# Output projections of two attentions split by heads, with sums, casts and subtractions put in another order

## The chip, the core and the metric

The kernel runs on one core of one Trainium2 chip. The metric is the time of one execution on the device in microseconds (us). Matmuls run on TensorE (PE in the profile), elementwise work on VectorE (DVE) and ScalarE (ACT); transfers from memory are started by SyncE (SP). Each engine takes its own instructions in a fixed order and waits, at the head of that order, for what an instruction needs.

## What is computed

Two transformer layers on 512 tokens of width 1024 in float32. Layer 0 has differential attention with 8 heads (the kernel calls two heads a pair), layer 1 sliding-window attention with 16 heads over 4 key/value heads and a learned sink. Each attention is followed by an output projection that is added to the stream x, then a normalization and a gated feed-forward block. Cut to what the change touches:

```python
a = p[:, :, 0] - lam * p[:, :, 1]                      # layer 0, per head
o = rms_norm(einsum('bhqk,bkhe->bqhe', a, v), subln) * (1.0 - lambda_init)
x = x + o.reshape(B, S, DA_V) @ w_o                    # "first end" below
h = rms_norm(x, ffn_norm[0]); x = x + swiglu(h, w_gate_up[0], w_down[0])
...
o = einsum('bnhgqk,bnkhd->bnqhgd', p, vw)              # layer 1, per unit
x = x + o.reshape(B, S, SW_HEADS * HEAD_DIM) @ sw_w_o  # "second end" below
h = rms_norm(x, ffn_norm[1]); x = x + swiglu(h, w_gate_up[1], w_down[1])
```

## The kernel before, in words

**Precision.** A float32 operand is kept as two tiles, a high part `hi` (a cast on ACT) and the rest `lo` (a subtraction on DVE, `src - hi`). `mm3` (L295 to L298) multiplies with three matmuls into one bank: hi by hi, hi by lo, lo by hi. So nearly every operand costs a cast on ACT and a subtraction on DVE before PE may use it. For activations that come out of a bank, `split_evac` (L300 to L303) does both; for weights, `load_w` (L280 on) does: one transfer (L287) into a tile `raw`, then a cast (L269) and a subtraction (L270) for each half. There are two `raw` buffers, so the transfer of a third piece starts when both subtractions of the first are done.

**Output projection.** `o_units` (L453) loads the four pieces of half of an output matrix, in the order (0,0), (0,1), (2,0), (2,1): the first number says which two of the half's four row blocks, the second which 512 columns. `o_block` (L457) makes one block of 128 tokens: for each half of the columns one bank, four `mm3`, and a sum on DVE that adds the bank to `xs`, the stream (L468). The first bank so needs the first and the third piece.

**Layer 0.** Four pairs of heads follow one another; `DA_STEPS3` is the table of places at which the last pair's steps (scores, weighted sum U, its weights W, norm N, and B, the spread of the inverse root `ro` over a bank by four small transposes, L1148) are put between the projection's matmuls. For pair 3 the projection of half 0 (pairs 0 and 1) fills first, then half 1 (pairs 2 and 3) for blocks 0 and 1; blocks 2 and 3 follow behind the table. The softmax of a block of tokens ends in four Exp on ACT (L1084) and two mixes on DVE (L1092); the mixed `s` is transposed (L1108) and split into `aT` (L302, L303) for the weighted sum. Then `ffn.norm(t)` (L520 on: Square on ACT, inverse root in small steps on DVE, two products `xn`, L532) and `ffn.turn(t)` (L534: two transposes of four 128x128 blocks, split into `hTh` and `hTl`) make block t ready for the feed-forward, whose `start` (L594 on) first multiplies blocks 0 and 1 (256 columns).

**Layer 1.** 16 units, each 4 heads on 128 queries, have five steps: turn the queries, scores, two transposes of the softmax (`turn_p`, L1439, split into `ph` and `pl`) and `weigh` (12 matmuls into `po`, split into `oh` and `ol`). `SW_AT` holds the five places of each unit. Units 14 and 15 end the table; the projection of token block 3 and the feed-forward of layer 1 follow.

**Order.** PE's order is that of the code. The order on ACT and DVE is made by a scheduler before the launch, from priorities (`high_priority`) and from the order in which things are written; `issue_after` forbids it to put an instruction ahead of a named one. SP starts transfers in its own order.

## Time and profile before

| | |
|---|---|
| three runs | 1122.44, 1122.76 and 1123.15 us, median 1122.76 |
| the profiled execution | 1122.68 us |
| its span (first to last instruction) | 1120.6 us |
| mean granted TensorE clock | 0.998 of full speed |
| busy share of PE, DVE, ACT, POOL | 98%, 90%, 63%, 5% |
| first end (last pair, projection) | about 225 to 270 us |
| second end (units 14 and 15, projection) | about 763 to 784 us |

The span lies 2.1 us below the time of its own execution. In a row of the timeline stand the start, the duration of one instruction (or of several alike from the first start to the last end), engine, line, operation, what it writes and reads, its shape, and in brackets how long the engine was idle before it and what released it. Durations of matmuls overlap: the distance from one start to the next is what a matmul takes on PE. The same holds on DVE and ACT for instructions that follow one another closely.

### The profile page before, as it was taken

The numbers are of one execution on the slowest core, as the hardware profiler recorded it, in microseconds if no ns is written. First come the engines' busy times: TensorE is split into PE (matmuls) and PEld (weight loads), VectorE is DVE, ScalarE is ACT, GpSimd is POOL, SyncE is SP. The second block draws the span as 40 slices with busy tenths as digits, with TensorE's granted clock in tenths as the row PEclk, the third lists the DMA queues.
The fourth block names the chain that finished last, engine by engine and source line by source line (L and its number), as shares of the span: only waits on it lengthen the run. The fifth ranks groups of instructions, "written<-read, shape, count | busy, mean of one in ns | idle before, by whom it ended". The sixth has DMA issues, their size and how long they took to land.

```text
span 1120.6 us, 20161 instructions
## 1 busy us (share of the span) xinstructions
PE 1101.9 (98%) x7206; PEld 979.5 (87%) x7206; DVE 1007.9 (90%) x2418; ACT 709.4 (63%) x1575; POOL 54.6 (5%) x76
## 2 busy tenths in 40 slices
PE   9999999999999999999999999999999999999998
PEld 7878888778989989989998778778989999998997
DVE  5979798979999999999998787988899999899997
ACT  5565756454556675675677499697555675566574
POOL 0100000000000010010003000000010000000000
PEclk9999999999999999999999999999999999999999
DMA  6312121224453444336124311120545247246213
GB/s 199 113 57 76 39 77 48 67 69 137 151 158 100 143 87 156 114 84 199 58 48 106 112 39 57 39 76 26 198 136 168 76 104 213 79 104 178 77 30 103
DMA packets 94085, 114.90 MB, mean 103 GB/s; under 512 B 5993, under 2 KB 70914, under 8 KB 93986
## 3 DMA queue, kind: packets, MB, share of 16 engines
q1 hardware_dynamic: 87216, 100.97, 28.0%
q0 software_dynamic: 6720, 12.65, 6.3%
q8 instruction: 56, 0.92, 0.3%
q14 instruction: 43, 0.35, 0.1%
q10 hardware_dynamic: 50, 0.01, 0.0%
HBM read 99.98 MB, written 2.10 MB: 91 GB/s over the span
## 4 chain that ended last, share of the span: by engine, by line
PE 81%; DVE 12%; ACT 6%; issue 1%; POOL 0%; DVEq 0%; ACTq 0%; POOLq 0%
PE acc L725 18%; PE tr L725 12%; PE tr L813 10%; PE acc L813 8%; PE acc L296 8%; PE acc L297 7%; PE acc L298 7%; PE po L725 2%; ACT s L1420 2%; PE tr L439 2%; DVE hss L389 1%; ACT s L1427 1%; DVE lo L270 1%; DVE u L405 1%; PE po L813 1%
## 5 line engine op out<-in xcount | busy, mean ns | idle before, releaser
L589 ACT CAST hi<-r 128x512 fp32r<-128x512 f32 x160 | 98.9, 620 | 78.9 <-PE acc L725 34.2
L296 PE MATMUL acc<-hi,hTh 128*128 128x512 f32 (+1 forms) x352 | 133.1, 378 | 2.2 <-DVE vl L1029 2.2
L297 PE MATMUL acc<-lo,hTh 128*128 128x512 f32 (+1 forms) x352 | 124.4, 354 | 0.4 <-DVE lo L270 0.4
L298 PE MATMUL acc<-hi,hTl 128*128 128x512 f32 (+1 forms) x352 | 124.4, 354 | 0.0
L589 ACT CAST hi<-g 128x512 fp32r<-128x512 f32 x154 | 94.9, 618 | 40.6 <-PE acc L297 19.2
L591 DVE TENSOR_TENSOR lo<-r,hi 128x512 fp32r<-128x512 f32 x160 | 104.8, 685 | 5.8 <-ACT hi L589 5.4
L589 ACT CAST hi<-raw 128x512 fp32r<-128x512 f32 x108 | 66.9, 620 | 61.5 <-PE tr L725 19.0
L796 ACT CAST ah<-lf 128x256 fp32r<-128x256 f32 x154 | 61.2, 404 | 47.2 <-PE tr L813 14.7
L725 PE MATMUL acc<-hTh,lo 128*128 128x256 f32 x288 | 81.5, 283 | 0.0
L725 PE MATMUL acc<-hTl,hi 128*128 128x256 f32 x288 | 81.5, 283 | 0.0
L725 PE MATMUL acc<-hTh,hi 128*128 128x256 f32 x288 | 81.4, 283 | 0.0
L725 PE MATMUL acc<-tl,hi 128*128 128x256 f32 x288 | 81.1, 282 | 0.0
L725 PE MATMUL acc<-th,hi 128*128 128x256 f32 x288 | 81.1, 281 | 0.0
L725 PE MATMUL acc<-th,lo 128*128 128x256 f32 x288 | 81.0, 281 | 0.0
L296 PEld LDWEIGHTS acc<-hi,hTh 128*128 128x128 f32 x352 | 66.9, 190 | 12.9 <-issue 2.6
L269 ACT CAST hi<-raw 128x512 fp32r<-128x512 f32 x96 | 57.4, 619 | 30.8 <-PE acc L298 17.6
L591 DVE TENSOR_TENSOR lo<-g,hi 128x512 fp32r<-128x512 f32 x110 | 75.2, 684 | 1.5 <-ACT hi L589 1.4
L298 PEld LDWEIGHTS acc<-hi,hTl 128*128 128x128 f32 x352 | 66.8, 190 | 9.5
L588 POOL DMA_DIRECT2D lo<-g x44 | 38.5, 975 | 715.1 <-ACT lo L587 308.4
L297 PEld LDWEIGHTS acc<-lo,hTh 128*128 128x128 f32 x352 | 67.1, 191 | 6.7 <-DVE lo L270 0.7
L591 DVE TENSOR_TENSOR lo<-raw,hi 128x512 fp32r<-128x512 f32 x108 | 72.7, 685 | 0.0
L270 DVE TENSOR_TENSOR lo<-raw,hi 128x512 fp32r<-128x512 f32 x96 | 64.4, 684 | 6.7 <-ACT hi L269 6.3
(278 smaller groups left out, 3635.0 us busy)
## 6 DMA issues: line engine op xcount, KB each, us to landing
r<-in_w_gate_up_dram SPq DMA_DIRECT2D x80, 512.0 KB, 4.9
g<-in_w_down_dram SPq DMA_DIRECT2D x88, 256.0 KB, 5.3
lo<-g POOLq DMA_DIRECT2D x44, 256.0 KB, 3.8
raw<-in_da_w_qkv_dram SPq DMA_DIRECT2D x30, 256.0 KB, 3.1
raw<-in_da_w_qkv_dram SPq DMA_DIRECT2D x8, 512.0 KB, 4.0
raw<-in_da_w_o_dram SPq DMA_DIRECT2D x8, 512.0 KB, 3.7
raw<-in_w_gate_up_dram SPq DMA_DIRECT2D x8, 512.0 KB, 3.7
raw<-in_sw_w_o_dram SPq DMA_DIRECT2D x8, 512.0 KB, 3.7
```

Of the source, the lines that this page charges most:

```text
L269: nc.scalar.copy(hi, part)
L270: nc.vector.tensor_tensor(lo, part, hi.bitcast(F32), op=ALU.subtract)
L296: nc.tensor.matmul(dst, sh, mh, start=start, stop=False)
L297: nc.tensor.matmul(dst, sh, ml, start=False, stop=False)
L298: nc.tensor.matmul(dst, sl, mh, start=False, stop=stop)
L439: nc.tensor.matmul(banks[c][:, cols], q[a][rows], k[b][rows], start=a + b == 0, stop=a == 1)
L588: nc.gpsimd.dma_start(out=lo.bitcast(F32), in_=src, accum_op=ALU.add)
L589: nc.scalar.copy(hi, src)
L591: nc.vector.tensor_tensor(lo, src, hi.bitcast(F32), op=ALU.subtract)
L725: nc.tensor.matmul(dst, l[:, k, :], r[:, k, :], start=fresh and k == 0 and i == 0, stop=k == 3 and i == 2, skip_group_check=not fresh)
L796: nc.scalar.copy(ah, src)
L813: nc.tensor.matmul(bank, l[:, tk], r, start=fresh and i == 0 and n == 0, stop=i == len(qs) - 1 and n == 2, skip_group_check=not fresh)
```

## The change

At the first end: the sums of two blocks of half 0, the casts and the subtractions of the four pieces of half 1 are held back, by `issue_after`. The sum (2, 1) waits for `rooted`, the step that makes `ro` for the first half of the tokens; the sum (3, 0) for `mixed`, the last mix of pair 3; the weights' casts for `raised`, the last Exp of pair 3, and their subtractions for `rooted`. Block 2 of half 1 is made with both banks open (`o_block2`): first the row blocks of pair 2 into both, then those of pair 3. The last B of `DA_STEPS3` goes one `mm3` later.

At the second end: `weigh` of unit 14 goes ahead of the first `turn_p` of unit 15 (two numbers of `SW_AT`: 77.7403 becomes 77.62 and 78.1612 becomes 77.64), `weigh` of unit 15 goes behind the first half of the first bank of the last projection block, which is `o_block2` too; `turn(0)` and `turn(1)` go behind one and two more `mm3` of that block's end; `norm(2)` is issued behind the last cast of unit 15, `norm(3)` as before behind the block. In PE's order it reads: `weigh` 14, `turn_p` 15 twice, half of bank 0, `weigh` 15, half of bank 1, `turn(0)`, the rest of bank 0, one `mm3` of bank 1, `turn(1)`, the last `mm3`.

```diff
--- before.py
+++ after.py
@@ -108,13 +108,13 @@
         (42.8, W, 1, 0),
         (43.3, W, 1, 1),
         (48.6, N, 1),
-        (56.9, B, 1),
+        (58.6, B, 1),
     ]
 
 
 DA_FILL3 = 0.4757
 SW_K = [11.4, 13, 18.5, 22]
...
 SW_R = [24.5925, 29, 34.7335, 50, 54, 60.3794]
 SW_F = 57.2488
 SW_BOOST = 51
@@ -247,7 +247,8 @@
             else:
                 eng.tensor_tensor(w, y, y, op=ALU.mult)
                 eng.scalar_tensor_tensor(w, w, -0.5, v, op0=ALU.mult, op1=ALU.mult)
-            eng.scalar_tensor_tensor(dst if it == 2 else y, w, 1.5, y, op0=ALU.add, op1=ALU.mult)
+            last = eng.scalar_tensor_tensor(dst if it == 2 else y, w, 1.5, y, op0=ALU.add, op1=ALU.mult)
+        return last
 
     class Split:
 
@@ -299,8 +300,9 @@
 
     def split_evac(hi, lo, src):
         with tc.high_priority(offset=pri["evac"]):
-            nc.scalar.copy(hi, src)
+            cast = nc.scalar.copy(hi, src)
             nc.vector.tensor_tensor(lo, src, hi.bitcast(F32), op=ALU.subtract)
+        return cast
 
     def new_hT():
         hh = xp.tile([P, KT, S], F32R, name=nm("hTh"), tag="hTh", bufs=1)
@@ -454,7 +456,7 @@
         return {(j, n): load_w([wv[:, k0 + j:k0 + j + 2, n * 512:(n + 1) * 512]], 2, 512)
                 for j in (0, 2) for n in range(2)}
 
-    def o_block(units, pieces, t, ready=None):
+    def o_block(units, pieces, t, ready=None, after=lambda t, n: None):
         while ready and not ready():
             yield None
         for n in range(2):
@@ -464,8 +466,24 @@
                 mm3(pt, sh, sl, *units[j - j % 2, n].row(j % 2), j == 0, j == 3)
                 yield 0.65
             xsl = xs[:, t, n * 512:(n + 1) * 512]
-            with tc.high_priority(offset=HOT):
+            with tc.high_priority(offset=HOT), ExitStack() as hold:
+                if after(t, n):
+                    hold.enter_context(tc.issue_after(after(t, n)))
                 nc.vector.tensor_tensor(xsl, xsl, pt, op=ALU.add)
+
+    def o_block2(units, pieces, t, order):
+
+        banks = {}
+        for n, half in order:
+            if n not in banks:
+                banks[n] = acc()
+            for j in (2 * half, 2 * half + 1):
+                mm3(banks[n], *pieces(j, t), *units[2 * half, n].row(j % 2), j == 0, j == 3)
+                yield n, j
+            if half:
+                xsl = xs[:, t, n * 512:(n + 1) * 512]
+                with tc.high_priority(offset=HOT):
+                    nc.vector.tensor_tensor(xsl, xsl, banks[n], op=ALU.add)
 
 
     class Flow:
@@ -1081,15 +1099,15 @@
             for h in range(2):
                 for c in range(2):
                     g = 2 * h + c
-                    nc.scalar.activation(sb[h][:, c, 0:n], sb[h][:, c, 0:n], AF.Exp, bias=mx[:, g:g + 1],
-                                         scale=self.scl[:, i, g:g + 1], accum_out=sm[:, g:g + 1])
+                    self.raised = nc.scalar.activation(sb[h][:, c, 0:n], sb[h][:, c, 0:n], AF.Exp, bias=mx[:, g:g + 1],
+                                                       scale=self.scl[:, i, g:g + 1], accum_out=sm[:, g:g + 1])
             rs = small([P, 2], "rs2")
             nc.vector.reciprocal(rs, sm[:, 1::2])
             cl = small([P, 2], "cl")
             nc.vector.scalar_tensor_tensor(cl, rs, nlam, sm[:, 0::2], op0=ALU.mult, op1=ALU.mult)
             for h in range(2):
                 p0, p1 = sb[h][:, 0, 0:n], sb[h][:, 1, 0:n]
-                nc.vector.scalar_tensor_tensor(p0, p1, cl[:, h:h + 1], p0, op0=ALU.mult, op1=ALU.add)
+                self.mixed = nc.vector.scalar_tensor_tensor(p0, p1, cl[:, h:h + 1], p0, op0=ALU.mult, op1=ALU.add)
             hf = i // 2
             if i % 2 == 0:
                 self.eps[hf] = small([P, 4], "eps", bufs=3)
@@ -1139,7 +1157,7 @@
                 nc.vector.scalar_tensor_tensor(so, pss[:, 0:8:2], 1.0 / P, self.eps[hf], op0=ALU.mult, op1=ALU.add)
             self.ro = small([P, 4], "ro")
             with tc.high_priority(offset=NPRI):
-                rsq(self.ro, so, 4)
+                self.rooted = rsq(self.ro, so, 4)
 
         def spread(self, hf):
             pb = att("po")
@@ -1235,11 +1253,18 @@
 
         da_units = {}
 
+        def after_da(t, n):
+            return {(2, 1): lambda: pairs[3].rooted.ins, (3, 0): lambda: pairs[3].mixed.ins}.get((t, n), lambda: None)()
+
         def o_da(half, ts, ready=None):
             if half not in da_units:
-                da_units[half] = o_units(da_w_o[0], 4 * half)
+                with ExitStack() as hold:
+                    if half:
+                        hold.enter_context(tc.issue_after(pairs[3].rooted.ins))
+                        hold.enter_context(tc.issue_after(pairs[3].raised.ins))
+                    da_units[half] = o_units(da_w_o[0], 4 * half)
             for t in ts:
-                yield from o_block(da_units[half], pieces_da(half), t, ready)
+                yield from o_block(da_units[half], pieces_da(half), t, ready, (after_da, lambda t, n: None)[half])
 
         late = []
         at = [0]
@@ -1264,7 +1289,7 @@
             fill.drain()
         ffn.norm(0)
         ffn.norm(1)
-        run(o_da(1, (2,)))
+        run(o_block2(da_units[1], pieces_da(1), 2, ((0, 0), (1, 0), (0, 1), (1, 1))))
         ffn.turn(0)
         ffn.norm(2)
         for n, _ in enumerate(o_da(1, (3,))):
@@ -1427,7 +1452,7 @@
                 nc.scalar.activation(sb[:, g, 0:n], sb[:, g, 0:n], AF.Copy, scale=rs[:, g:g + 1])
             soft[u] = sb
 
-        pT, soft, kdone, vdone = {}, {}, set(), set()
+        pT, soft, casts, kdone, vdone = {}, {}, {}, set(), set()
 
         def turn_p(u, b):
             s, i, kk, kv, blocks = place(u)
@@ -1439,7 +1464,7 @@
                 nc.tensor.transpose(pt[:, col:col + P], soft[u][:, g, b * P:(b + 1) * P], ident)
             ph = ap.tile([P, 512], F32R, name=nm("ph"), tag="ph", bufs=2)
             pl = ap.tile([P, 512], F32R, name=nm("pl"), tag="pl", bufs=2)
-            split_evac(ph, pl, pt)
+            casts[u, b] = split_evac(ph, pl, pt)
             pT[u, b] = (ph, pl)
 
         def weigh(u):
@@ -1470,7 +1495,7 @@
             if ch not in sw_units:
                 sw_units[ch] = o_units(sw_w_o[0], 4 * ch)
             yield from o_block(sw_units[ch], pieces_sw(ch), t)
-            if ch:
+            if ch and t < 2:
                 ffn.norm(t)
 
         def hook(k, t):
@@ -1499,7 +1524,7 @@
         todo = [(at, t, turn_a) for t, at in enumerate(SW_K)]
         for u in range(16):
             for n, f in enumerate((turn_q, score, turn_p, turn_p, weigh)):
-                if u >= 4 or n:
+                if (u >= 4 or n) and (u, n) != (15, 4):
                     todo.append((SW_AT[5 * u + n], u, f) + ((n - 2,) if n in (2, 3) else ()))
         todo += [(at, *z, q_rope) for at, z in zip(SW_R, (("B", 1), ("B", 2), ("B", 3), ("C", 1), ("C", 2), ("C", 3)))]
         todo.append((SW_F, Ffn))
@@ -1519,11 +1544,17 @@
             else:
                 z[1](z[0], *z[2:])
         fill.drain()
-        for n, _ in enumerate(o_sw(1, 3)):
-            if n == 1:
+        last = casts[15, 1]
+        for n, j in o_block2(sw_units[1], pieces_sw(1), 3, ((0, 0), (1, 0), (0, 1), (1, 1))):
+            if (n, j) == (0, 1):
+                weigh(15)
+            if (n, j) == (1, 1):
+                with tc.issue_after(last.ins):
+                    ffn.norm(2)
                 ffn.turn(0)
-            if n == 5:
+            if (n, j) == (1, 2):
                 ffn.turn(1)
+        ffn.norm(3)
         ffn.start({1: lambda: ffn.turn(2), 3: lambda: ffn.turn(3)})
 
     with tc.tile_pool(name="ffn1", bufs=1, reuse_waits="tile") as fp:
```

Line numbers behind the first hunks are one to 31 larger in the changed kernel (L270 becomes L271, L303 becomes L304, L468 becomes L472, or L486 in `o_block2`). The orders on SP and POOL are the same in both. Three places on DVE show what moves. In the rows a name ends in its numbers; the first of them is used in the text.

First end, DVE, before: `lo_656` and `lo_658` are the two subtractions of the first piece of half 1 (`raw_654`), `rsq` and `ro` the steps of the inverse root, `osb` and `eps` the pair's next norm.

```order
L250 SCALAR_TENSOR_TENSOR rsq_s_628_3027<-rsq_t_629_3028,rsq_s_628_3027 128x4
L1080 SCALAR_TENSOR_TENSOR mx_615_2974<-mx_615_2974,hscl_492_2419 128x4
L270 TENSOR_TENSOR lo_656_3178<-raw_654_3175,hi_655_3177 128x512
L248 TENSOR_TENSOR rsq_t_629_3028<-rsq_s_628_3027 128x4
L270 TENSOR_TENSOR lo_658_3182<-raw_654_3175,hi_657_3181 128x512
L249 SCALAR_TENSOR_TENSOR rsq_t_629_3028<-rsq_t_629_3028,so_626_3024 128x4
L250 SCALAR_TENSOR_TENSOR ro_627_3026<-rsq_t_629_3028,rsq_s_628_3027 128x4
L1149 SCALAR_TENSOR_TENSOR osb_622_3004<-osb_622_3004,gsub_86,po_640_3088 128x512
L468 TENSOR_TENSOR xs_76<-xs_76,acc_634_3066 128x512
```

And now, some 20 rows further on; `aT` and `tr` are the split of the last mixes' transposes, `raw_664` is the third piece, which takes the buffer of `raw_654`.

```order
L304 TENSOR_TENSOR aT_646_3104<-tr_647_3105,aT_644_3102 128x128
L304 TENSOR_TENSOR aT_637_3078<-tr_650_3130,aT_635_3076 128x2x128
L472 TENSOR_TENSOR xs_76<-xs_76,acc_648_3114 128x512
L304 TENSOR_TENSOR aT_646_3104<-tr_649_3118,aT_644_3102 128x2x128
L304 TENSOR_TENSOR aT_638_3079<-tr_650_3130,aT_636_3077 128x2x128
L271 TENSOR_TENSOR lo_656_3178<-raw_654_3175,hi_655_3177 128x512
L271 TENSOR_TENSOR lo_658_3182<-raw_654_3175,hi_657_3181 128x512
L271 TENSOR_TENSOR lo_661_3188<-raw_659_3185,hi_660_3187 128x512
L271 TENSOR_TENSOR lo_663_3192<-raw_659_3185,hi_662_3191 128x512
L271 TENSOR_TENSOR lo_666_3198<-raw_664_3195,hi_665_3197 128x512
```

The first piece's subtractions have moved from between the steps of `ro` to behind the last `aT`; those of the second and third piece follow at once.

Start of the feed-forward of layer 0, DVE, before: `hTl_687<-tr_712` and `<-tr_713` are the two halves of `turn(1)`, `xs<-acc_711` is the last sum of the projection, `frr_706` the end of the inverse root of `norm(2)`.

```order
L270 TENSOR_TENSOR lo_727_3477<-raw_725_3474,hi_726_3476 128x512
L246 TENSOR_SCALAR rsq_t_708_3390<-rsq_s_707_3389,rsq_h_709_3391 128x1
L270 TENSOR_TENSOR lo_729_3481<-raw_725_3474,hi_728_3480 128x512
L250 SCALAR_TENSOR_TENSOR rsq_s_707_3389<-rsq_t_708_3390,rsq_s_707_3389 128x1
L303 TENSOR_TENSOR hTl_687_3303<-tr_712_3421,hTh_686_3302 128x4x128
L246 TENSOR_SCALAR rsq_t_708_3390<-rsq_s_707_3389,rsq_h_709_3391 128x1
L468 TENSOR_TENSOR xs_76<-xs_76,acc_711_3417 128x512
L250 SCALAR_TENSOR_TENSOR rsq_s_707_3389<-rsq_t_708_3390,rsq_s_707_3389 128x1
L303 TENSOR_TENSOR hTl_687_3303<-tr_713_3428,hTh_686_3302 128x4x128
```

And now; `xn_705` are the products of `norm(2)`, `fss_714` is the first step of `norm(3)`, which takes the result of its Square on ACT.

```order
L271 TENSOR_TENSOR lo_727_3477<-raw_725_3474,hi_726_3476 128x512
L250 SCALAR_TENSOR_TENSOR rsq_s_707_3389<-rsq_t_708_3390,rsq_s_707_3389 128x1
L271 TENSOR_TENSOR lo_729_3481<-raw_725_3474,hi_728_3480 128x512
L246 TENSOR_SCALAR rsq_t_708_3390<-rsq_s_707_3389,rsq_h_709_3391 128x1
L304 TENSOR_TENSOR hTl_687_3303<-tr_712_3421,hTh_686_3302 128x4x128
L250 SCALAR_TENSOR_TENSOR frr_706_3388<-rsq_t_708_3390,rsq_s_707_3389 128x1
L472 TENSOR_TENSOR xs_76<-xs_76,acc_711_3417 128x512
L550 SCALAR_TENSOR_TENSOR xn_705_3385<-xs_76,frr_706_3388,gb_539_2671 128x512
L550 SCALAR_TENSOR_TENSOR xn_705_3385<-xs_76,frr_706_3388,gb_540_2673 128x512
L545 TENSOR_SCALAR fss_714_3445<-fss_714_3445 128x1
L304 TENSOR_TENSOR hTl_687_3303<-tr_713_3428,hTh_686_3302 128x4x128
```

The second half of `turn(1)` has moved behind the last sum, the products of `norm(2)` and the first step of `norm(3)`.

Second end, DVE, before: `tr_2010` and `tr_2011` are `turn(0)`, `tr_2013` and `tr_2014` are `turn(1)`, `raw_2026` and `raw_2031` are the second and third of the four first pieces of the feed-forward's weights.

```order
L303 TENSOR_TENSOR hTl_1939_9616<-tr_2010_9940,hTh_1938_9615 128x4x128
L303 TENSOR_TENSOR hTl_1939_9616<-tr_2011_9947,hTh_1938_9615 128x4x128
L468 TENSOR_TENSOR xs_76<-xs_76,acc_2009_9933 128x512
L270 TENSOR_TENSOR lo_2028_10021<-raw_2026_10018,hi_2027_10020 128x512
L270 TENSOR_TENSOR lo_2030_10025<-raw_2026_10018,hi_2029_10024 128x512
L303 TENSOR_TENSOR hTl_1939_9616<-tr_2013_9968,hTh_1938_9615 128x4x128
L303 TENSOR_TENSOR hTl_1939_9616<-tr_2014_9975,hTh_1938_9615 128x4x128
L468 TENSOR_TENSOR xs_76<-xs_76,acc_2012_9961 128x512
```

And now; both sums of the last block stand together, `raw_2036` is the fourth piece, `fss_2015` the first step of `norm(3)`.

```order
L486 TENSOR_TENSOR xs_76<-xs_76,acc_2000_9897 128x512
L486 TENSOR_TENSOR xs_76<-xs_76,acc_2004_9921 128x512
L271 TENSOR_TENSOR lo_2033_10031<-raw_2031_10028,hi_2032_10030 128x512
L271 TENSOR_TENSOR lo_2035_10035<-raw_2031_10028,hi_2034_10034 128x512
L271 TENSOR_TENSOR lo_2038_10041<-raw_2036_10038,hi_2037_10040 128x512
L545 TENSOR_SCALAR fss_2015_9989<-fss_2015_9989 128x1
L271 TENSOR_TENSOR lo_2040_10045<-raw_2036_10038,hi_2039_10044 128x512
L241 TENSOR_SCALAR rsq_h_2020_9996<-fss_2015_9989 128x1
L242 TENSOR_SCALAR rsq_t_2019_9995<-fss_2015_9989 128x1
L304 TENSOR_TENSOR hTl_1939_9616<-tr_2013_9971,hTh_1938_9615 128x4x128
L243 TENSOR_SCALAR rsq_s_2018_9994<-rsq_t_2019_9995 128x1
L304 TENSOR_TENSOR hTl_1939_9616<-tr_2014_9978,hTh_1938_9615 128x4x128
```

`turn(1)`'s subtractions have moved behind four subtractions of weights and the first step of `norm(3)`.

More of the change, by code (lines that the diff above doesn't have):

```diff
@@ L116 @@
 SW_K = [11.4, 13, 18.5, 22]
-SW_AT = [11.99, 12, 15.9293, 17.8936, 24.5, 15.49, 15.5, 20.5, 21.3936, 26, 19.99, 20, 25, 26, 28.8496, 24.49, 24.5, 29.5, 30.5, 33.0389, 25.6, 29.3765, 35.7519, 36, 38.8496, 28.8, 30.9738, 38.2, 40.3017, 42.0496, 32, 34.1738, 41.4, 43.5017, 45.2496, 36.9539, 39.3779, 46.3539, 48.4383, 50.2036, 45.6745, 48.0985, 55.0745, 57.0527, 58.1744, 47.0802, 52.5434, 56.4802, 57.4802, 60.3298, 50.3802, 54.7802, 59.7802, 60.7802, 63.6298, 53.6802, 58.0802, 63.0802, 64.0802, 66.9298, 57.032, 60.327, 66.3802, 67.3802, 70.2298, 60.4435, 63.7903, 69.8435, 70.8435, 72.7553, 65.4286, 69.8286, 74.8286, 75.8286, 77.7403, 67.7612, 72.1612, 77.6383, 78.1612, 80.073]
+SW_AT = [11.99, 12, 15.9293, 17.8936, 24.5, 15.49, 15.5, 20.5, 21.3936, 26, 19.99, 20, 25, 26, 28.8496, 24.49, 24.5, 29.5, 30.5, 33.0389, 25.6, 29.3765, 35.7519, 36, 38.8496, 28.8, 30.9738, 38.2, 40.3017, 42.0496, 32, 34.1738, 41.4, 43.5017, 45.2496, 36.9539, 39.3779, 46.3539, 48.4383, 50.2036, 45.6745, 48.0985, 55.0745, 57.0527, 58.1744, 47.0802, 52.5434, 56.4802, 57.4802, 60.3298, 50.3802, 54.7802, 59.7802, 60.7802, 63.6298, 53.6802, 58.0802, 63.0802, 64.0802, 66.9298, 57.032, 60.327, 66.3802, 67.3802, 70.2298, 60.4435, 63.7903, 69.8435, 70.8435, 72.7553, 65.4286, 69.8286, 74.8286, 75.8286, 77.62, 67.7612, 72.1612, 77.6383, 77.64, 80.073]
 SW_R = [24.5925, 29, 34.7335, 50, 54, 60.3794]
```

## The prediction

> **What bounds the kernel now.** I read the page first, then the chain of waits, then the timeline of PE, DVE and ACT at the two ends. The busy shares and the chain's shares:
>
> ```profile
> PE 1101.9 (98%) x7206; PEld 979.5 (87%) x7206; DVE 1007.9 (90%) x2418; ACT 709.4 (63%) x1575; POOL 54.6 (5%) x76
> ...
> PE 81%; DVE 12%; ACT 6%; issue 1%; POOL 0%; DVEq 0%; ACTq 0%; POOLq 0%
> ```
>
> PE is busy for 1101.9 of 1120.6 us, so only about 19 us can be had without taking matmuls out, and this change takes none out. DVE at 90% is the second engine: what is put behind something on it comes late soon. The change is therefore worth what PE's waits at the ends are worth, minus new waits. PE's waits there, from its timeline:
>
> ```profile
> 235.05 0.62 PE L1148 MATMUL po<-ident,ro 128*128 128x128 f32 x4 [0.96 <-DVE ro L250]
> 238.56 0.66 PE L1108 MATMUL tr<-ident,s 128*128 128x128 f32 x4 [1.15 <-DVE s L1092]
> 252.00 0.39 PE L298 MATMUL acc<-hi,ol 128*128 128x512 f32 x1
> 252.75 0.62 PE L1148 MATMUL po<-ident,ro 128*128 128x128 f32 x4 [0.37 <-DVE ro L250]
> 773.46 0.60 PE L1439 MATMUL tr<-ident,s 128*128 128x128 f32 x4
> 774.82 0.39 PE L296 MATMUL po<-ph,vpad 128*128 128x256 f32 x1 [0.76 <-DVE ol L303]
> ```
>
> Waits of 0.96, 1.15, about 0.5 (matmuls of 512 columns start some 0.23 apart, so PE was free at 252.23 and began at 252.75) and 0.76 us: 3.4 us in all. That is what the change can get.
>
> **First end, what goes.** DVE before the first wait, and ACT:
>
> ```profile
> 233.28 0.68 DVE L270 TENSOR_TENSOR lo<-raw,hi 128x512 fp32r<-128x512 f32 x1
> 233.96 0.68 DVE L270 TENSOR_TENSOR lo<-raw,hi 128x512 fp32r<-128x512 f32 x1
> 234.75 0.16 DVE L250 SCALAR_TENSOR_TENSOR ro<-rsq_t,rsq_s 128x4 f32<-128x4 f32 x1
> ...
> 232.44 1.30 ACT L269 CAST hi<-raw 128x512 fp32r<-128x512 f32 x2 [4.05 <-PE acc L298]
> 233.65 0.81 ACT L1084 ACTIVATE s<-s,mx,hscl 128x512 f32<-128x512 f32 x1
> ```
>
> The two subtractions take about 1.2 us out of the chain of `ro`; the two casts hold the four Exp back by 1.2 us, of which about 0.8 can be had, since `s` is ready only then. So the 0.96 goes and `s` comes up to 0.8 earlier. The rest of the path to the next bank (mix, transposes, `aT`, weighted sum) runs on DVE, which stays packed. Bounds: PE enters the first bank of half 1 between 0 and 0.8 us earlier; I take 0.5, since the wait for `s` behind the one for `ro` absorbs part.
>
> **First end, what comes.** In the new order the first piece's two subtractions, `lo_656` and `lo_658`, stand behind the last `aT`. The third piece takes their buffer, and its transfer starts when they end. Before (transfers of `raw` at this end; DVE; PE's first bank; the casts of a late piece):
>
> ```profile
> L287 SPq DMA_DIRECT2D raw<-in_da_w_o_dram x2: 368/368/368, 234.7 to 243.5; - x2
> ...
> DMA to landing us min/median/max: 3.4/3.6/4.8
> ...
> 243.31 0.42 DVE L303 TENSOR_TENSOR aT<-tr,aT 128x256 fp32r<-128x256 f32 x1
> 243.64 1.28 DVE L270 TENSOR_TENSOR lo<-raw,hi 128x512 fp32r<-128x512 f32 x2
> ...
> 244.40 0.45 PE L296 MATMUL acc<-hi,oh 128*128 128x512 f32 x1
> ...
> 245.83 0.39 PE L296 MATMUL acc<-hi,oh 128*128 128x512 f32 x1
> ...
> 247.07 1.14 ACT L269 CAST hi<-raw 128x512 fp32r<-128x512 f32 x2 [1.16 <-DMA raw<-in_da_w_o_dram]
> ```
>
> The third piece's transfer started at 234.7, at the end of the 233.96 subtraction; the fourth at 243.5 was landed, cast and used without a wait. Now: the last `aT` ended at 243.65 with two weight subtractions of 0.60 each between the `aT` steps; without these it ends about 242.5 (an estimate: 1.2 less). Two subtractions (1.28) end at 243.8; landing by the median 3.6, at 247.4; one cast of 0.62, at 248.0. PE needs the third piece at its third `mm3`: 245.83, six matmuls (0.24 each) behind 244.40, less 0.5: 245.3. It waits 2.7 us. The first matmul then runs 0.23, while the subtraction takes 0.68: another 0.45. So from 245.83 PE is behind by 248.0 − 245.83 + 0.45 = 2.6. The wait at 252.75 (0.5) lies behind that, and its transposes also come one `mm3` later: it goes. The first end is worth +2.6 − 0.5 = +2.1. By the landings of 3.4 and 4.8 this is +1.9 to +3.3; the fourth piece starts 1.2 us behind the third and is needed behind six `mm3` more, so it is hidden.
>
> **Start of the feed-forward of layer 0.** PE, DVE and ACT before:
>
> ```profile
> 270.02 0.28 PE L296 MATMUL acc<-hTh,hi 128*128 128x256 f32 x1
> 271.74 0.29 PE L297 MATMUL acc<-hTl,hi 128*128 128x256 f32 x1
> ...
> 270.23 0.68 DVE L468 TENSOR_TENSOR xs<-xs,acc 128x512 f32<-128x512 f32 x1
> 270.90 0.69 DVE L303 TENSOR_TENSOR hTl<-tr,hTh 128x512 fp32r<-128x512 f32 x1
> 272.00 1.42 DVE L532 SCALAR_TENSOR_TENSOR xn<-xs,frr,gb 128x512 f32<-128x512 f32 x2
> ...
> 270.95 1.06 ACT L526 ACTIVATE xn<-xs 128x1024 f32<-128x1024 f32 x1 [2.15 <-DVE xs L468]
> 271.92 0.18 ACT L526 ACTIVATION_READ_ACCUMULATOR xn<-xs 128x1 f32 x1
> ```
>
> Before, the second half of `turn(1)` followed the last sum, at 270.90 to 271.6. Now `fss_714` stands ahead of it and needs the Square, which needs the sum: 270.95 to 272.1. Then `fss` 0.15 and its own 0.68: about 272.9. PE wants it at its fourteenth matmul, the row at 271.74: a wait of 1.2 us. The products `xn` stand ahead too, but run while the Square does. The first half of `turn(1)`, ahead of the sum, stands behind the weights' subtractions still, and if these come late it delays the sum and the Square with it: 0 to 0.7 (one subtraction, 0.68) more; I take 0.4. Together +1.6, and the first end with this start +3.7.
>
> **Second end.** Here the order puts `turn(1)`'s subtractions behind four subtractions of weights and behind `fss_2015`. PE, DVE, ACT before, and the transfers of the weights:
>
> ```profile
> 772.01 0.69 DVE L303 TENSOR_TENSOR pl<-tr,ph 128x512 fp32r<-128x512 f32 x1 [0.78 <-ACT ph L302]
> 783.61 0.28 PE L296 MATMUL acc<-hTh,hi 128*128 128x256 f32 x1
> ...
> 781.01 1.29 DVE L270 TENSOR_TENSOR lo<-raw,hi 128x512 fp32r<-128x512 f32 x2
> 782.62 1.29 DVE L303 TENSOR_TENSOR hTl<-tr,hTh 128x512 fp32r<-128x512 f32 x2 [0.33 <-ACT hTh L302]
> ...
> 782.00 1.07 ACT L302 CAST hTh<-tr 128x512 fp32r<-128x512 f32 x2 [1.18 <-PE tr L314]
> 784.54 1.06 ACT L526 ACTIVATE xn<-xs 128x1024 f32<-128x1024 f32 x1 [0.26 <-DVE xs L468]
> 785.96 1.14 ACT L269 CAST hi<-raw 128x512 fp32r<-128x512 f32 x2 [0.27 <-DMA raw<-in_w_gate_up_dram]
> ...
> L287 SPq DMA_DIRECT2D raw<-in_w_gate_up_dram x2: 367/368/368, 779.3 to 782.3; - x2
> ```
>
> Before, `turn(1)`'s subtractions followed right behind its casts, 782.62 behind 782.00, and behind two subtractions of weights (781.01); the Square came later, at 784.54. What goes: the 0.76 at 774.82, because other matmuls stand there; weighing unit 14 still waits for `pl` (772.70), so no more than that is had; I take 0.7. PE reaches the feed-forward about 782.9 instead of 783.61. What comes: its first matmul needs `hTh` of `turn(1)`, its second `hTl`. `weigh` 14 ends at 773.5, where the transposes began before. On ACT stand behind it one `oh` and two `ph` (together about 1.5, an estimate from 1.07 for two casts), a Square (1.06 + 0.18) and the first piece's casts (1.14): 777.4. With one subtraction behind them, 0.68, the first buffer is free about 778.2, and 3.6 later, at 781.8, the third piece lands. The fourth needs the subtractions of the second piece, one of whose `hi` waits for a tile that the first half of bank 1 gives back: 773.5, eight transposes 0.7, six matmuls of 512 columns 1.4, twelve of 256 1.5 and six of 512 1.4 make 778.5; with cast and subtraction 780.1, landing at 783.8. ACT then casts the third piece (to 783.0), `turn(1)` (784.1), the fourth (785.25) and makes the Square of `norm(3)` (786.5). DVE: `fss` 0.15, the last subtraction 0.6, small steps 0.15, `hTl` 0.68: 788.1. PE, there at 782.9, would have begun its second matmul at 783.0 and waits 5.0 in all, some of it for `hTh`. Net −0.7 + 5.0 = +4.3. Bounds, by where the Square stands: if the fourth piece's casts end a microsecond sooner, +3.3; by landings of 4.8, +5.5. Sum of both ends 3.7 + 4.3 = +8.0.
>
> **The clock behind these waits.** The longest wait before, its first matmul behind it, and the granted clock (next to last but one number) in stretches:
>
> ```profile
> 46.70 0.79 PE L296 MATMUL acc<-hi,hTh 128*128 128x512 f32 x1 [2.16 <-DVE vl L1029]
> 50.02 0.48 PE L296 MATMUL acc<-hi,hTh 128*128 128x512 f32 x1
> ...
> 46.00:48.00 2.00, 1.30 (x3) 1.11 (x4) 2.00 (x7) 0.82 (x3) 0.00 (x0) 0.63 0.11 38
> 48.00:50.00 2.00, 2.00 (x8) 1.51 (x8) 2.00 (x4) 0.40 (x1) 0.00 (x0) 0.52 0.00 0
> 50.00:54.00 4.00, 4.00 (x24) 3.11 (x24) 3.30 (x9) 1.22 (x2) 0.00 (x0) 1.00 0.82 250
> ```
>
> An idle time of 2.16 us brought the clock to 0.52 until about 50. In 46.70 to 50.02, 3.32 us, what PE did would at full clock have taken 0.52 of it: 3.32 × 0.48 = 1.6. The first 0.2 ran at a mean of 0.63 with idle time in it, so I take 1.5. The waits of 2.7 and 5.0 are longer than 2.16, the 1.2 is shorter; the waits of about 1 us above dropped nothing (the mean granted clock is 0.998). So I add 2 × 1.5 = 3.0. [...]
>
> **The sum.** 3.7 + 4.3 + 3.0 = +11.0. The profiled execution, 1122.68 us, is its span of 1120.6 and 2.1 around it; the median of the three runs is 1122.76, the same within 0.1. 1122.7 + 11.0 = 1133.7 us.
>
> **The rivals.** (1) The waits come, the clock drops once or not at all: 1133.7 − 1.5 = 1132.2 or − 3.0 = 1130.7. [...] (2) Only one end pays: the third piece or `hTl` comes early enough. First end alone, 1122.7 + 3.7 + 1.5 − 0.7 = 1127.2; second alone, 1122.7 + 4.3 + 1.5 − 0.5 = 1128.0. For it: both rest on one chain each through landings. (3) The other side, the hold is covered: if the first piece's subtractions slip between the `aT` steps' waits on ACT and the third piece is landed and cast by 245.3, which needs its transfer started by 245.3 − 0.6 − 3.6 = 241.1 instead of 243.8, and `hTl` doesn't stand behind the Square, then only what goes counts: −0.5 (−0.8 at best), −0.5, −0.7: −1.7 to −2.0, 1120.7. Against it: the rows of the order say plainly that both `lo` stand behind the last `aT` and `hTl` behind `fss`. (4) More than forecast: the 1.2 at the feed-forward's start, which the late first half can lengthen to 1.9, drops the clock as well, 1135.2. That the change doesn't do what it says is excluded by the rows shown.
>
> **The numbers.** Forecast 0.45; rival 1 0.26; rival 2 0.11; rival 3 0.12, half of it the same and half faster, as −2.0 stands near the bound; rival 4 0.06. A measurement of this kernel can tell about 0.2%, 2.25 us, from no change. So faster 0.06, same 0.06, slower 0.88. The range reaches from rival 2's lower end, 1127.0, to rival 4 with the later landings, 1136.5.
>
> **What would show it.** In the profile after: PE about 245 to 248 idle for a cast or subtraction of weights (L270, L271), with the third transfer at about 243.8 in place of 234.7; no wait at L1148's successor; a wait of 1 to 2 us about 274 for `hTl`; a wait of about 5 us for `hTl` at the start of the second feed-forward, with half clock for about 3 us behind it. Wrong it is if the third piece's transfer starts before 241, or if those waits stay under 1 us.

## The result and the profile after

The changed kernel takes 1137.7 us (median of six runs, 1133.38 to 1139.25), the kernel before 1122.95 us beside it (1122.29 to 1127.8). The ratio of the changed kernel to before, which is that of the means (1136.9 to 1124.1), is 1.0114, 95% interval [1.0092, 1.0137]: slower, by 10.3 to 15.4 us on 1122.8. The forecast was 1133.7 us, with a range of 1127.0 to 1136.5. 1.0114 times the 1122.76 of before is 1135.6, inside it; the median of 1137.7 is above it by 1.2. The six runs differ in their mean granted clock: four have 0.991 or 0.992 and take 1136.92 to 1139.25 us, two have 0.995 and take 1133.38 and 1134.64. The profiled execution, 1138.48 us, is one of the four.

The span went from 1120.6 to 1136.5 us, 15.9 more. PE's waits in the profile after, from the view of waits (engine, what it ran, who released it, us, times, longest):

```profile
PE acc L298 <- DVE rsq_s L243: 4.3, 1, 4.3
PE acc L297 <- ACT hi L270: 2.9, 1, 2.9
PE acc L297 <- DVE vl L1047: 2.2, 1, 2.2
...
PE acc L298 <- DVE hTl L304: 1.4, 2, 1.0
PE tr L1126 <- DVE s L1110: 1.4, 1, 1.4
...
PE acc L297 <- ACT hTh L303: 0.8, 1, 0.8
```

The 2.2 stood before too. The 2.9 is new at the first end, the 1.4 in two parts at the start of the first feed-forward, the 0.8 and the 4.3 at the start of the second; no wait for `ro` is listed any more. The name `rsq_s` of the longest is the instruction that ended last on the releasing side; what the product reads is `hTl`.

**First end.** PE, DVE and ACT around the 2.9, and the transfers of `raw`:

```profile
237.96 0.66 PE L1126 MATMUL tr<-ident,s 128*128 128x128 f32 x4 [1.39 <-DVE s L1110]
...
239.51 0.63 PE L1126 MATMUL tr<-ident,s 128*128 128x128 f32 x4 [0.20 <-DVE aT L304]
...
242.63 0.38 PE L298 MATMUL po<-aT,vh 128*128 128x256 f32 x1 [0.29 <-DVE aT L304]
...
244.66 0.44 PE L297 MATMUL acc<-hi,oh 128*128 128x512 f32 x1
...
249.14 0.80 PE L297 MATMUL acc<-hi,oh 128*128 128x512 f32 x1 [2.88 <-ACT hi L270]
249.87 0.79 PE L298 MATMUL acc<-lo,oh 128*128 128x512 f32 x1
...
242.82 2.49 DVE L271 TENSOR_TENSOR lo<-raw,hi 128x512 fp32r<-128x512 f32 x4
249.12 2.06 DVE L271 TENSOR_TENSOR lo<-raw,hi 128x512 fp32r<-128x512 f32 x3 [3.81 <-ACT hi L270]
...
248.47 1.14 ACT L270 CAST hi<-raw 128x512 fp32r<-128x512 f32 x2 [2.31 <-DMA raw<-in_da_w_o_dram]
...
L288 SPq DMA_DIRECT2D raw<-in_da_w_o_dram x2: 367/367/367, 244.2 to 245.4; - x2
...
DMA to landing us min/median/max: 3.4/4.0/4.4
```

The chain reads from the bottom up: the third piece's transfer starts at 244.2 (234.7 before), because the first two of the four subtractions that begin at 242.82 end there; the casts wait for it to 248.47, PE for the cast to 249.14. Before, PE made this product at 245.83: 3.3 us lost.

The granted clock in the stretch behind it, and behind the longest wait. A line has the stretch and its length, the busy time and number of instructions of PE, its weight loads, DVE, ACT and POOL, then the granted clock (third number from the end), the busy share of DMA and GB/s:

```profile
248.00:250.00 2.00, 0.86 (x2) 0.42 (x2) 0.88 (x2) 1.30 (x3) 0.00 (x0) 0.68 0.50 180
250.00:258.00 8.00, 8.00 (x23) 6.65 (x24) 3.62 (x12) 0.98 (x2) 0.00 (x0) 0.50 0.43 131
258.00:260.00 2.00, 2.00 (x8) 1.54 (x8) 0.78 (x3) 0.09 (x1) 0.00 (x0) 0.76 0.00 0
...
794.00:796.00 2.00, 0.00 (x0) 0.00 (x0) 1.45 (x3) 1.61 (x3) 0.00 (x0) 0.72 1.08 382
796.00:800.00 4.00, 1.86 (x8) 1.86 (x9) 3.21 (x13) 0.58 (x2) 0.00 (x0) 0.50 1.09 382
800.00:802.00 2.00, 2.00 (x13) 2.00 (x12) 1.54 (x3) 0.00 (x0) 0.00 (x0) 0.58 1.08 397
```

The clock drops at 248.7, still in the wait, and PE works at 0.50 from 249.1 to about 258.9. That alone is (258.9 − 249.1) × 0.5 = 4.9 us, more than the wait that brought it on. Behind the second wait PE works at 0.50 from 798.1 to about 801.7: 1.8 us.

**Start of the first feed-forward.** PE, DVE and ACT:

```profile
277.59 0.28 PE L297 MATMUL acc<-hTh,hi 128*128 128x256 f32 x1
278.31 0.39 PE L298 MATMUL acc<-hTl,hi 128*128 128x256 f32 x1 [0.44 <-DVE hTl L304]
280.96 0.39 PE L298 MATMUL acc<-hTl,hi 128*128 128x256 f32 x1 [0.96 <-DVE hTl L304]
...
280.17 0.14 DVE L545 TENSOR_SCALAR fss<-fss 128x1 f32<-128x1 f32 x1
280.23 0.68 DVE L304 TENSOR_TENSOR hTl<-tr,hTh 128x512 fp32r<-128x512 f32 x1
...
278.95 1.06 ACT L544 ACTIVATE xn<-xs 128x1024 f32<-128x1024 f32 x1 [2.58 <-DVE xs L472]
```

The second `hTl` stands right behind `fss`, `fss` behind the Square, as the order said. From the first product to the fourteenth PE takes 3.37 us, 1.72 before: +1.65.

**Second end.** The same engines:

```profile
793.45 0.39 PE L297 MATMUL acc<-hTh,hi 128*128 128x256 f32 x1 [0.75 <-ACT hTh L303]
798.14 0.58 PE L298 MATMUL acc<-hTl,hi 128*128 128x256 f32 x1 [4.30 <-DVE rsq_s L243]
...
796.61 0.15 DVE L545 TENSOR_SCALAR fss<-fss 128x1 f32<-128x1 f32 x1 [0.88 <-ACT xn L544]
796.68 0.68 DVE L271 TENSOR_TENSOR lo<-raw,hi 128x512 fp32r<-128x512 f32 x1
797.41 0.68 DVE L304 TENSOR_TENSOR hTl<-tr,hTh 128x512 fp32r<-128x512 f32 x1
...
791.77 1.14 ACT L270 CAST hi<-raw 128x512 fp32r<-128x512 f32 x2 [1.95 <-DMA raw<-in_w_gate_up_dram]
792.82 1.06 ACT L303 CAST hTh<-tr 128x512 fp32r<-128x512 f32 x2
794.39 1.14 ACT L270 CAST hi<-raw 128x512 fp32r<-128x512 f32 x2 [0.51 <-DMA raw<-in_w_gate_up_dram]
795.44 1.05 ACT L544 ACTIVATE xn<-xs 128x1024 f32<-128x1024 f32 x1
```

ACT waits for the third piece, casts it, then `hTh`, waits for the fourth, casts it, squares; DVE waits for each in turn, and `hTl` comes last, at 797.41.

The account of this execution: PE began the first feed-forward 277.59 − 270.02 = 7.6 us late, 4.9 of it clock; 1.65 at its start makes 9.2; from there to the second product of the second feed-forward (783.61 + 0.12 before, 798.14 now) 14.4 − 9.2 = 5.2; 1.8 of clock. In all 16.2, against 15.9 between the spans.

### The profile page after: what moved, and what is told of

The parts are those of the page before. It is cut to its first block, busy times and chain, and to the rows that moved or that the text cites. A ratio compares the mean times of both kernels' runs of the same rounds, so it can differ in the third digit from the quotient of the medians.

```text
span 1136.5 us, 20160 instructions
## 1 busy us (share of the span) xinstructions
PE 1109.2 (98%) x7206; PEld 984.9 (87%) x7206; DVE 1009.0 (89%) x2418; ACT 709.6 (62%) x1575; POOL 54.4 (5%) x76
## 4 chain that ended last, share of the span: by engine, by line
PE 80%; DVE 11%; ACT 6%; DMA 1%; issue 1%; POOL 0%; DVEq 0%; ACTq 0%; SPq 0%; POOLq 0%
PE acc L743 18%; PE tr L743 11%; PE tr L831 9%; PE acc L831 8%; PE acc L297 8%; PE acc L298 7%; PE acc L299 7%; PE po L743 2%; PE tr L441 2%; ACT s L1445 2%; DVE lo L271 1%; DVE hss L391 1%; ACT s L1452 1%; PE tr L428 1%; DVE u L407 1%
## 5 line engine op out<-in xcount | busy, mean ns | idle before, releaser
L270 ACT CAST hi<-raw 128x512 fp32r<-128x512 f32 x96 | 57.0, 619 | 30.2 <-PE acc L299 13.5
L271 DVE TENSOR_TENSOR lo<-raw,hi 128x512 fp32r<-128x512 f32 x96 | 64.4, 684 | 8.2 <-ACT hi L270 7.9
```

Of the source, the lines that this page charges most:

```text
L270: nc.scalar.copy(hi, part)
L271: nc.vector.tensor_tensor(lo, part, hi.bitcast(F32), op=ALU.subtract)
```

## The experiments

The time given is the median. Each ratio is that of the means, to the kernel before in runs on the same chip, with its 95% interval; between runs on different chips only ratios are compared.

**Is each end's loss its own?** The first end of the change alone, and the second end alone. The first is the changed kernel with the second end put back; the edit in short:

```diff
-        for n, j in o_block2(sw_units[1], pieces_sw(1), 3, ((0, 0), (1, 0), (0, 1), (1, 1))):
...
+        for n, _ in enumerate(o_sw(1, 3)):
+            if n == 1:
+                ffn.turn(0)
+            if n == 5:
+                ffn.turn(1)
```

(with the two numbers of `SW_AT` and `weigh(15)` at their old places).

> Only the first end of the change (holds on sums and weights, two open banks in block 2, the last B one product later); the second end as before. Theory: the changed trace lost 7.6 us up to the first matmul of the first feed-forward (270.02 to 277.59), 4.9 of it as half clock (about 9.8 us at 0.50), and 1.65 more at that feed-forward's start; the second end's loss is its own. So this kernel is slower than before by 4.3 (no clock drop) to 9.3 us, 1127 to 1132, and its trace has the wait of about 2.9 us for a weight's cast, the third transfer at about 244, and no wait over 1.5 us at the second end. Rival: the second end's wait of 4.3 is an after-effect of the first end's lateness; then it shows here too, and the time is 1133 or more.

1129.88 us, ratio 1.0062 [1.0044, 1.008]. Its waits have 3.1 us for a weight's cast, the 1.4 for `hTl`, and none over 0.8 at the second end. The third piece's transfer starts at 244.1.

The second end alone takes out both holds, the later B and the two open banks of the first end:

```diff
-        (58.6, B, 1),
+        (56.9, B, 1),
...
-                yield from o_block(da_units[half], pieces_da(half), t, ready, (after_da, lambda t, n: None)[half])
+                yield from o_block(da_units[half], pieces_da(half), t, ready)
...
-        run(o_block2(da_units[1], pieces_da(1), 2, ((0, 0), (1, 0), (0, 1), (1, 1))))
+        run(o_da(1, (2,)))
```

(and the `hold` around `o_units`).

> Only the second end of the change (unit 14 weighed first, unit 15 inside the last block, norms put behind); the first end as before. Theory: -0.6 for the wait that goes, +5.5 for the low halves of turn(1) that stand behind four subtractions of weights and the first step of the last norm, +1.75 for half clock: +6.7, 1129.4, and up to 3 us more if the clock stays low for longer, as at the first end. The trace has a wait of 4 to 5 us at the second feed-forward's start and none over 1.2 us at the first end. Rival: the wait is an after-effect of the first end; then this kernel is within 1 us of before.

1131.34 us, ratio 1.007 [1.0053, 1.0086]. Its waits at the second end:

```profile
PE acc L298 <- DVE rsq_s L243: 5.1, 1, 5.1
PE po L297 <- ACT ph L303: 0.6, 1, 0.6
PE acc L297 <- ACT hTh L303: 0.4, 1, 0.4
```

Both rivals fall: each end has its own loss. The two ratios add up to 1.0132, and the whole change has 1.0114 [1.0092, 1.0137].

**Which hold makes the first wait?** One run leaves out the hold on the weights:

```diff
-                with ExitStack() as hold:
-                    if half:
-                        hold.enter_context(tc.issue_after(pairs[3].rooted.ins))
-                        hold.enter_context(tc.issue_after(pairs[3].raised.ins))
-                    da_units[half] = o_units(da_w_o[0], 4 * half)
+                da_units[half] = o_units(da_w_o[0], 4 * half)
```

> The changed kernel without the hold on the casts and subtractions of half 1's weights; the holds on the two sums stay. Theory: what delays the third transfer is that the second subtraction of the first piece stands behind the last aT, and in this kernel's order it still does (the first one is ahead, the second behind): transfer at about 244, wait of 2 to 3 us, time as the changed kernel's, 1133 to 1139. Rival: the hold on the weights alone makes the wait; then the transfer starts about 235 to 239, the wait is gone with its half clock, and the time is 3 to 8 us below the changed kernel's.

1135.82 us, ratio 1.0106 [1.0091, 1.0122]; wait 2.6 us, third transfer at 242.2 (in this profile the half clock near 47 us is missing, so that its first end stands 1.4 us earlier than in the changed kernel's). The other leaves out the hold on the two sums:

```diff
-                yield from o_block(da_units[half], pieces_da(half), t, ready, (after_da, lambda t, n: None)[half])
+                yield from o_block(da_units[half], pieces_da(half), t, ready)
```

> The changed kernel without the holds on the two sums of half 0; the hold on the weights of half 1 stays. Theory: the weights' hold alone puts the first piece's subtractions late: transfer at about 244, wait of 2 to 3 us, time as the changed kernel's, 1133 to 1139. Rival: only the sums' hold makes the wait; then the wait and its half clock are gone here, 3 to 8 us below the changed kernel's. If both this run and the one without the weights' hold keep the wait, each of the two holds is enough by itself.

1135.64 us, ratio 1.0111 [1.0083, 1.0139]; wait 1.9 us, third transfer at 243.4. So either hold is enough by itself. The third run leaves out both:

> The changed kernel without either hold at the first end (sums and weights); the two open banks of block 2, the later B, and the whole second end stay. Theory: the first end's wait of 2.9 and its half clock are gone, third transfer at about 234; the waits for turn(1)'s low halves at the first feed-forward's start (1.4) stay if the later B or block 2 makes them, and the second end's +6.7 to +8 stays: 1130 to 1132.5, 3 to 7 us below the changed kernel. Rival: the two open banks of block 2 carry the first end's loss; then the time stays at 1134 to 1138.

1131.0 us, ratio 1.0069 [1.0055, 1.0083]. Its transfers of `raw` at the first end, and its waits there:

```profile
L288 SPq DMA_DIRECT2D raw<-in_da_w_o_dram x2: 368/368/368, 234.8 to 243.6; - x2
...
PE acc L298 <- DVE hTl L304: 1.4, 2, 1.0
PE tr L1126 <- DVE s L1110: 1.2, 1, 1.2
PE po L1166 <- DVE ro L250: 0.9, 1, 0.9
```

The transfer is back at 234.8, the wait for the cast is gone and the clock at the first end is 1.00; the old waits for `s` and `ro` are back. Its ratio is that of the second end alone (1.007), though it has the two open banks of the first end. So the rival, that these carry the first end's loss, falls. The 1.4 for `hTl` is still there, so the holds don't make it.

**What makes the waits at the first feed-forward's start?** The kernel before with one number changed, the last B one product later (56.9 to 58.6 in `DA_STEPS3`).

> The kernel before with one number changed: the last B of the table one product later (56.9 to 58.6). Theory: the waits of 0.44 and 0.96 us for the low halves of turn(1) at the first feed-forward's start belong to this number (they stood without the holds as long as B was late, and were gone with B early), not to the two open banks: they show here, 1.65 us by the changed kernel's rows, less the wait for ro that goes (0.5): 0.5 to 1.5 us slower than before, 1.0004 to 1.0014. Rival: they come from the two open banks; then no wait over 0.3 us there and the time is up to 0.5 us below before.

1123.83 us, ratio 1.0009 [1.0, 1.0018]. Its waits:

```profile
PE acc L297 <- DVE vl L1047: 2.2, 1, 2.2
PE acc L298 <- DVE hTl L304: 1.4, 2, 1.0
PE tr L1126 <- DVE s L1110: 1.2, 1, 1.2
PE po L1166 <- DVE ro L250: 1.0, 1, 1.0
```

The 1.4 comes with the number: four transposes go one product later on PE, and some 20 us on the second `hTl` stands right behind `fss` (271.11 and 271.18), as in the changed kernel. How the scheduler comes to that order no run shows. The second wait for `ro` is gone (one is listed where there were two). The interval touches 1, and ten of the eleven runs have a granted clock of 0.998, against 14 of the 27 of before: at 0.998 the means are 1124.09 and 1123.80 us. So the time doesn't show the loss; the trace does.

**Is the half clock from the idle time?** The first end of the change alone, and on PE, ahead of the product that waits for the third piece, 30 transposes of the identity into a bank that nobody reads:

```diff
+                if busy_at and busy_at == [(t, n, j)]:
+                    busy(busy_at.pop() and 30)
                 mm3(pt, sh, sl, *units[j - j % 2, n].row(j % 2), j == 0, j == 3)
```

> The kernel with only the first end changed, and 30 transposes of the identity (some 0.09 us each, 2.7 us, their result unused) put on PE ahead of the product that waits for the third piece, where the changed kernel's trace has 2.9 us of idle time. Theory: the half clock of 3 to 10 us comes from that idle time; filled, the clock stays at 1.00, the wait for data stays as long, and the time is 1.5 to 4.9 us below the run with only the first end (ratio 1.0062 to before), that is 1.002 to 1.005 times before: 1125.5 to 1128. Rival: the half clock has another cause (the change of load behind the wait); then it stays, and with 2.7 us of extra work the time is the same or above 1130.

1126.45 us, ratio 1.0032 [1.0021, 1.0044], against 1.0062 [1.0044, 1.008] without them. PE's timeline with them:

```profile
244.97 3.44 PE L220 MATMUL po<-ident 128*128 128x128 f32 x30
248.16 0.47 PE L298 MATMUL acc<-hi,oh 128*128 128x512 f32 x1
248.70 0.50 PE L299 MATMUL acc<-lo,oh 128*128 128x512 f32 x1
249.04 0.40 PE L300 MATMUL acc<-hi,ol 128*128 128x512 f32 x1
```

The data come as late (the third transfer starts at 243.0, and ACT waits 3.1 us in all for the two transfers, 2.8 without the transposes), the wait is filled with work that does nothing, and the matmuls behind it start 0.54 and 0.34 apart instead of 0.73 and 0.60 in the changed kernel (249.14, 249.87 and 250.47); the granted clock of this profile is 1.00 throughout. All six runs have 0.998 or 1.000, where the four without the transposes have 0.994 to 0.997. The half clock is thus from the idle time, and was worth 0.3% here. The rival, that the load behind the wait brings it on, falls.

**Does the place of `turn(1)` make the second wait?** The changed kernel with the casts and subtractions of `turn(1)` at a higher priority:

```diff
             if (n, j) == (1, 2):
+                pri["evac"] = 200
                 ffn.turn(1)
+                pri["evac"] = SW_EVAC
```

> The changed kernel with turn(1) at the second end given a higher priority, so that its casts and subtractions stand ahead of those of the third and fourth piece and of the last norm's first step; nothing else moves before. Theory: the wait of 4.3 us for the low half falls to 0 to 1, the third piece's product may wait a little more, and no half clock follows: 3 to 6 us below the changed kernel, 1130 to 1133. Rival: the weights themselves are late (their transfers land in 4.3 us), so PE only waits for another piece in place of the low half, and the time stays within 2 us of the changed kernel's.

1131.55 us, ratio 1.008 [1.0066, 1.0095]. Its waits at the second end:

```profile
PE acc L297 <- ACT hTh L303: 0.7, 1, 0.7
PE po L297 <- ACT ph L303: 0.6, 1, 0.6
PE acc L298 <- DVE hTl L304: 0.4, 1, 0.4
PE po L298 <- DVE pl L304: 0.3, 1, 0.3
```

4.3 has become 0.4, with no half clock behind it, and no wait for a piece has taken its place. The late weights were not the limit; the order was.

**All mended.** The changed kernel without the holds, with B at 56.9, and `turn(1)` at (0, 2) in place of (1, 2) with the higher priority.

> The changed kernel with all that the theory blames undone: no holds at the first end, B at its old place, turn(1) at the second end one product earlier and at the higher priority; the two open banks at both ends and unit 14 weighed first stay. Theory: no wait over 1.3 us, no half clock, and of the intended gain what is left at the second end, 0.5 us, against small new waits there: 1122 to 1124.5, within 0.2% of before. Rival: splitting the banks by heads costs by itself (accumulation over two open banks, sums that come together at the end), then it stays above 1126.

1124.2 us, ratio 1.0007 [0.9997, 1.0016]. No wait over 1.2 us at either end. What stays of the change, the open banks and unit 14 weighed first, gains nothing that can be measured.

**A wait that stood before.** The kernel before with 20 transposes in its 2.2 us wait at 44.5 to 46.7:

```diff
                 each = DA_FILL
+                if not p:
+                    busy(20)
```

> The kernel before, with 20 transposes of the identity (about 1.8 us, result unused) put on PE into its one wait over 2 us, at 44.5 to 46.7, and nothing else. Of ten profiles so far six show one stretch of half clock of 3.4 us behind that wait (1.7 us lost), four none. Theory: a wait of 2.2 us drops the clock in some executions only; filled it never does, so the mean falls by about 0.6 x 1.7 = 1.0 us and the spread of the runs narrows: 0.9985 to 1.0000 times before. Rival: the spread of before comes from elsewhere; then the ratio is 1.000 to 1.002 by the fill's own cost.

1122.08 us, ratio 0.9994 [0.9985, 1.0003]; the clock at 46 to 50 is 1.00, and none of the 11 runs has a granted clock below 0.999. Of the 27 runs of before, 14 have 0.998 and a mean of 1123.80 us, 12 have 1.000 and 1122.49; the filled kernel's mean is 1122.33. So the fill takes away a drop that costs about 1.3 us in half of the runs. The whole mean is lower by 0.7, with 1.0 expected, and the interval still holds no change: a small gain is likely and not shown by the time. The same in the mended kernel:

> The mended change (no holds, B at its old place, turn(1) earlier and ahead) with the same fill. Theory: 1.0 us below the mended kernel (1.0007 times before), so 0.999 to 1.0005: the version that beats both if the fill is worth its 1.0 us. Rival: the fill costs as much as it saves, 1.0005 to 1.002.

1122.26 us, ratio 0.9991 [0.9982, 1.0]. By the two ratios it beats the changed kernel by over 1%; against before its interval ends at 1, so a gain is not shown.

## Why the prediction was right, and where it was off

The waits were forecast from the orders and rows, and came where they were named: 2.7 us for the third piece's cast (2.9 measured, transfer forecast at 243.8, measured 244.2); 1.6 at the first feed-forward's start (1.65); 5.0 at the second one's (0.75 + 4.30). Both half clocks came. The side, slower, was right, and so was the reason.

The term that was mis-sized is the clock: 2 × 1.5 = 3.0 forecast, 4.9 + 1.8 = 6.7 measured in this execution. The 1.5 was read from one stretch of 3.4 us in before, and taken for the price of any drop. The prices come in steps, below; a wait of 2.9 us here brought three of them. The filled run shows that term by itself.

That the time came so near is in part luck. In the profiled execution the loss is 16.2 us, 5 more than the 11.0 forecast: 3.7 of that is clock, the rest small misses. The two runs at a clock of 0.995, with about half as much half clock, lie within 1 us of the 1133.7.

The 2.7 us agree better than their parts: PE came to the third piece at about 246.1 instead of 245.3, and the piece was late too: its transfer started 0.4 us later than forecast and its cast 4.3 us behind that (248.47) instead of 3.6. At the second end the loss net of the gain was 5.2 where 4.3 was forecast: the 0.7 that should have been saved was not. The wait of 0.76 for `ol` went, and waits of 0.63 for `ph` and 0.34 for `pl` came.

Two small steps were wrong. PE was to enter the first bank of half 1 0.5 us earlier; it came 0.26 later (244.66 for 244.40). The transposes of `s` did start 0.60 earlier (237.96 for 238.56: the wait for `ro` is gone, the one for `s` rose from 1.15 to 1.39), but behind them PE waits twice for `aT` (0.20 and 0.29), where it didn't before: the work on DVE, not the casts, set this path. And the prediction put the late subtractions down to the order without saying which line of the change makes it; there are two, each enough alone. The waits at the first feed-forward, which it took for part of the projection's rearrangement, hang on the one number of B.

Of the rivals none came true. Both drops came, behind both waits; one end alone was not what happened; the hold was not covered; the 1.4 at the first feed-forward dropped nothing (the clock from 260 on is 1.00).

Where did the gain go that the change could have had? The waits for `ro` went, 0.96 and 0.5, and the 0.76 at the second end; the waits for `s`, `aT`, `ph` and `pl` took most of it back. DVE is 90% busy, and an instruction taken out of one chain stands in another.

What stays open: one drop at the first end lasts 3.4 us and another 10.2, behind waits of 1.9 to 3.1 us whose length does not sort them (3.4 behind 2.6 and 3.1 us, 10.2 behind 1.9, 2.9 and 3.1). What does sort them was not shown.

## What to carry to other kernels

Before holding an instruction back, follow its buffer: a subtraction that is late by itself harms nobody, but it gave back the buffer for the third piece, and the wait appeared 5 us on, at another engine. On a full engine read the whole order around the place, since a hold, a priority or a step of PE's own table moves neighbours it does not name. And price an idle gap of TensorE with the half clock that may come behind it: here gaps of 1.9 to 5.1 us brought 3.4 to 10.2 us of it (the one of 2.2 us in six profiles of eleven), and behind the 2.9 us at the first end it cost 4.9 us, more than the gap. Where the gap can't be closed, work that does nothing can keep the clock, as 30 transposes kept it at 1.00 here.

## What the runs showed of the hardware

The half clock comes in steps. For each profile, the stretch of half clock behind a wait of PE, added up from stretches of half a microsecond, or of 2 and 4 us for late B alone (the missing share of the clock times the stretch, doubled):

| wait | in the profiles of | length of half clock, us |
|---|---|---|
| 2.2 us at 46 (also in before) | before, after, first end alone, no sum hold, no holds, mended | 3.4 each |
| the same 2.2 us | second end alone, no weight hold, `turn(1)` first, fill at the first end, late B alone | 0 each |
| 2.6 and 3.1 us, first end | no weight hold, first end alone | 3.4 each |
| 1.9, 2.9, 3.1 us, first end | no sum hold, after, `turn(1)` first | 10.2 each |
| 4.3 to 5.1 us, second end | after, second end alone, no weight hold, no sum hold, no holds | 6.8 each |

All are 0, 1, 2 or 3 times 3.4 us. In the profile of the changed kernel they last 3.41, 10.24 and 6.83 us and begin at 47.35, 248.73 and 794.86. PE's waits end there at 46.87, 249.14 and 798.14: two of the drops begin inside the wait, one 0.5 us behind it. From one beginning to the next it is 201.38 and 546.13 us, which is 59.0 and 160.0 times 3.413 (a third of the 10.24). The four other profiles with more than one drop show the same: 59.0 (first end alone), 159.0 (no weight hold), 59.0 and 160.0 (no sum hold), 217.0 (no holds). Against the work the drops lie differently in each profile: with the same wait of 2.2 us they begin between 46.51 and 47.65.

PE's busy time just ahead goes with the drops. In the 3.41 us ahead of each of 16 drops, in nine profiles, PE was busy for 0.3 to 1.6 us; for the six with the wait at 46 it was 1.2 to 1.4. In five profiles that wait dropped nothing. Three of these have a drop later on; stretches of 3.41 us counted back from it cut the wait in two, and the emptier stretch holds 1.8, 1.7 and 1.9 us of work (second end alone, no weight hold, `turn(1)` first). That the place of a wait decides is the author's reading of these cases; no run moved a wait to test it. Filled, the 2.2 us dropped the clock in neither of two profiles (1.00 from 46 to 54).

How long a drop lasts is seen in part. At the second end the wait of 4.3 to 5.1 us goes on into the first of the two steps, in which PE is busy for 0.1 to 1.7 us of 3.41. At the first end PE is busy for 2.7, 3.0 and 3.3 us of the first step in the three long drops, for 3.1 and 3.4 in the two short ones: this does not sort them.
